# Low weight halves kept in DRAM, narrow products in a gated recurrence, and two deferred parts at another place

## The chip, the cores and the metric

The kernel runs on one core of one Trainium2 chip. The metric is the device time of one execution in microseconds (us). Engines are called PE (TensorE, matrix products), DVE (VectorE), ACT (ScalarE), POOL (GpSimd) and SP (SyncE, which only issues DMAs here).

## What is computed

Two sequences, a sample of 512 tokens and a prompt of 256, each of width 1024, go through the same two layers, all in float32:

```python
def trunk(x, ...):
    for l in range(DEPTH):                       # 2
        if l == 0: mix = ab_mixer(x, ...)        # HGRN heads beside dilated attention, output product
        else:      mix = conv_mixer(x, ...)      # gated product, 31-tap depthwise convolution
        x = layer_norm(ALPHA * x + mix, ...)
        x = layer_norm(ALPHA * x + sq_relu_mlp(x, mlp_w1[l], mlp_w2[l]), ...)

def sq_relu_mlp(x, w1, w2):
    return jnp.square(jax.nn.relu(x @ w1)) @ w2  # 1024 -> 4096 -> 1024

def conv_mixer(x, ...):
    a, gate = jnp.split(x @ w_in + b_in, 2, axis=-1)
    u = depthwise_conv(a * jax.nn.sigmoid(gate), dw_w, 31 taps) + dw_b
    return jax.nn.silu(layer_norm(u, n_g, n_b)) @ w_out + b_out
```

The HGRN mixer is a gated linear recurrence in both directions, over four heads of 128 channels: the state is decayed by a gate f and fed with k v at each token, and read with q.

## The kernel before

**Segments.** The sample is the long segment (`TS` = 512 columns, tiles 0 to 3, `segs` = `(0,)`), the prompt the short one (`TP` = 256, tiles 4 and 5, `segs` = `(1,)`). Most steps take one of them.

**Split products.** Weights and activations are split into a rounded high half (`wh`, `x0h`, `x1h`) and the low rest (`wl`, `x0l`, `x1l`), and a product is the sum of three: high by high, high by low, low by high. Weights come in units of 128 x 1024 (512 KB). `plan_units` lists them in the order of use. `advance` (lines 138 to 148) loads a unit into `raw` on SP's queue (line 143, three buffers), makes `wh` on ACT (line 135) and `wl` by a subtraction (line 136) on DVE, or on POOL for the units in `self.onpool`; these are all units from the convolution's first input product up to the second layer's MLP of both segments. `wh` and `wl` have five buffers each. `unit` hands one out and has the next three issued.

**HGRN.** For each head, `hgrn` builds the attention-like matrix `at` level by level for steps s of 1, 2, 4, ... 64 (`LEVELS`). At a level PE multiplies the keys by the queries (line 760 for s under 16, line 768 for s = 16, line 774 above), DVE copies the entries of that level from PSUM into `at` under a mask (line 778), and then `advance` of that function (lines 735 to 737) multiplies queries, keys and gate totals on, the forward direction on DVE and the backward one on POOL. For s under 16 a level is one product of 128 x 128 for each of six chunks, into a PSUM tile of its own, though the mask takes entries inside blocks of 2 s only. For s of 16 and more the products go to blocks inside one tile per segment (`ptop`). The input products of the next head run between the levels.

**First MLP layer.** `DEFER` is 8, so all eight chunks are first done for the long segment alone (from about 600 to 930 us), and then again for the short one, in twelve deferred parts: for each two chunks c and c+1 an `up c` (four units, products on line 168; ReLU and square on ACT, lines 940 to 942; the low half on DVE, line 943), an `up c+1`, and a `pair c` (eight units, products on line 980, sums on DVE, line 242). Each of the 64 units is so loaded and split twice.

**Where the parts stand.** `steps` writes the order: `MIX` says how many parts follow the first norm's middle and each two input products (`cin`) of the long segment's convolution, `NPOS` how many stand between the convolution's `center` and `norm` steps. What is left stands behind `norm`. The order before is: first norm with up 0; two `cin`, up 1, pair 0; two `cin`, up 2, up 3; two `cin`, pair 2; two `cin`, up 4, up 5, pair 4, up 6; `center`; up 7; `norm`; pair 6; then the short segment's norm and the output product `cout`. This order is a priority: a scheduler in the compiler builds each engine's queue by it and by when it reckons that the operands are there. `LOW` puts the convolution's taps 500 places back.

**Convolution.** 31 taps a channel tile on DVE (line 1021, the last on 1018), a running sum over tiles (line 1027). `do_center`: PE forms the mean (line 1037), DVE subtracts it (1041), ACT squares (1043), POOL and DVE add the squares (1048). `do_norm`: PE sums (1060), ACT takes the root (1064), DVE makes a diagonal (1067), PE spreads it (1070), and `channel_silu` (1079 to 1083, then the split into `x0h` and `x0l`) makes the operand of `cout` (line 182). The transposes of the norms are on line 232.

Of the kernel before, what the change touches and what calls it, by code (L numbers as in the profile page):

```python
# [20 lines left out]
P = 128  # L21
D = 1024
# [23 lines left out]
MIX = (1, 2, 2, 1, 4)  # L46
CMIX = (5,)
PT = "s"
NPOS = (0, 1)
# [51 lines left out]
class Kernel:  # L101
    def __init__(self, tc, ins, outs, ctx):
        self.tc, self.nc, self.i, self.o, self.ctx = tc, tc.nc, ins, outs, ctx
        self.n = 0
        self.post = False
        self.turn = 0
        self.mark = None
        self.flight = []
        self.x = [None, None]
        self.plan = []  # L110
        self.ready = {}
        self.issued = 0
        self.taken = 0
# [24 lines left out]
    def advance(self, upto):  # L138
        nc = self.nc
        while self.issued < min(upto, len(self.plan)):  # L140
            key, src = self.plan[self.issued]
            raw = self.sb(self.wp, [P, D], "raw", F32, RAW)
            nc.sync.dma_start(raw, src)
            hi = self.sb(self.wp, [P, D], "wh", F32R, WH)
            lo = self.sb(self.wp, [P, D], "wl", F32R, WL)
            self.split(raw, hi, lo, nc.gpsimd if self.issued in self.onpool else None)
            self.ready[self.issued] = (key, hi, lo)
            self.issued += 1
# [113 lines left out]
    def plan_units(self):  # L262
# [32 lines left out]
        self.onpool = set()  # L295
        win = False
        for step in self.steps():
            n0 = len(pl)
            if step[0] == "cin":
                win = True  # L300
            if step[2] == (0, 1):
                win = False
            {"up": up, "down": down, "pair": pair, "cin": conv_in, "cout": conv_out}.get(step[0], lambda *_: None)(*step[1])
            if win:
                self.onpool.update(n0 + q for q in range(len(pl) - n0))
# [402 lines left out]
    def hgrn(self, h, qs, ks, fs, gs, v):  # L708
# [31 lines left out]
        ptop = None  # L740
        for li, s in enumerate(LEVELS):
# [5 lines left out]
            for seg, (lo, hi) in enumerate(segs):  # L747
                if low or ptop is None or len(ptop) < 2:
                    pl = self.ps("s")
                    if not low:  # L750
                        ptop = (ptop or []) + [pl]
                else:
                    pl = ptop[seg]
                for c in range(lo, hi):
                    cc = slice(c * P, (c + 1) * P)
                    po = pl[:, (c - lo) * P : (c - lo + 1) * P]
                    if low:
                        rhs = bass.AP(tensor=qq.tensor, offset=qq.offset + c * P,
                                      ap=[qq.ap[0], [2 * s, P // (2 * s)], [T + s, 2], [1, s]])
                        nc.tensor.matmul(po, kc[:, cc], rhs, start=True, stop=True)  # L760
                        continue
# [438 lines left out]
```

## Time and profile before

| | us |
|---|---|
| median of 3 runs | 1906.98 (1906.2 to 1912.15) |
| profiled execution | 1907.15 |
| its span, first to last instruction | 1905.1 |
| granted clock of TensorE, mean | 0.987 |
| PE busy in the span | 1844.4 |
| DVE busy | 1146.5 |
| ACT busy | 738.2 |
| POOL busy | 603.3 |

Busy times of PE are modelled ends of pipelined products, so a busy PE can still be slow: the granted clock has to be read beside it. 1.00 is the level of 2.4 GHz, and a mean below 1.00 means that part of the stretch ran at 1.2 GHz.

### The profile page before, as it was taken

The page shows a single profiled execution, that of the slowest core. Times are in us where ns is not written, and L with a number is a line of the kernel's source. Part 1 is how long each engine was busy: PE and PEld are TensorE (multiplying, and loading weights), DVE is VectorE, ACT ScalarE, POOL GpSimd, SP SyncE. Part 2 cuts the span into 40 slices and gives each one's busy share as a digit, 9 for nine tenths or more (in the row PEclk, how much of TensorE's full clock was granted, in tenths as well). Part 3 has the DMA queues.
Part 4 walks back from the last instruction along what each step waited for, and adds up shares of the span by engine and source line. Part 5 has one row for each costly group of instructions (what it writes and reads, how often), then busy time and mean ns, then how long its engine had stood idle before and what let it go on. Part 6 is the DMA issues. An engine that isn't in the chain of part 4 may idle for free.

```text
span 1905.1 us, 26155 instructions
## 1 busy us (share of the span) xinstructions
PE 1844.4 (97%) x10516; PEld 1569.5 (82%) x10516; DVE 1146.5 (60%) x1813; ACT 738.2 (39%) x1200; POOL 603.3 (32%) x368
## 2 busy tenths in 40 slices
PE   8999999999999999999999999898999999999998
PEld 6798788887788888888789898688888789888886
DVE  4533527766766434334879999979993744333336
ACT  4423322334215333333444345544434545423322
POOL 4000105544310000000376668566445667000003
PEclk9999989999999999999999999899999999999999
DMA  7122221111213333333254444353332346321211
GB/s 234 34 72 74 65 89 45 34 45 35 100 48 122 107 93 92 108 100 95 72 157 149 148 145 155 122 155 107 94 99 89 129 159 194 116 67 59 64 44 66
DMA packets 56300, 189.57 MB, mean 100 GB/s; under 512 B 6979, under 2 KB 10099, under 8 KB 56180
## 3 DMA queue, kind: packets, MB, share of 16 engines
q1 hardware_dynamic: 52196, 177.23, 30.0%
q0 software_dynamic: 3120, 7.53, 1.4%
q10 hardware_dynamic: 864, 3.15, 0.5%
q8 instruction: 82, 1.34, 0.3%
q14 instruction: 38, 0.31, 0.1%
HBM read 182.49 MB, written 5.38 MB: 99 GB/s over the span
## 4 chain that ended last, share of the span: by engine, by line
PE 85%; DVE 11%; ACT 1%; issue 1%; POOL 1%; DMA 1%; SPq 0%; DVEq 0%; ACTq 0%; POOLq 0%
PE g L168 44%; PE s L182 25%; PE g L182 7%; PE s L980 3%; DVE qq L735 1%; DVE at L778 1%; DVE w L1082 1%; DVE x0l L136 1%; DVE g L736 1%; DVE r L242 1%; DVE x1l L136 1%; ACT wh L135 0%; DVE g L737 0%; DVE w L1083 0%; PE s L531 0%
## 5 line engine op out<-in xcount | busy, mean ns | idle before, releaser
L135 ACT ACTIVATE wh<-raw 128x1024 fp32r<-128x1024 f32 x320 | 339.2, 1061 | 731.8 <-PE g L168 304.8
L136 POOL TENSOR_TENSOR wl<-raw,wh 128x1024 fp32r<-128x1024 f32 x168 | 411.2, 2457 | 224.1 <-ACT wh L135 223.9
L182 PE MATMUL s<-wh,t 128*128 128x512 f32 x1280 | 398.1, 389 | 1.5 <-DVE r L242 1.5
L168 PE MATMUL g<-x0h,wh 128*128 128x512 f32 x864 | 339.6, 394 | 9.5 <-ACT wh L135 7.7
L168 PE MATMUL g<-x0l,wh 128*128 128x512 f32 x864 | 338.8, 392 | 0.2 <-DVE x0l L136 0.2
L168 PE MATMUL g<-x0h,wl 128*128 128x512 f32 x864 | 338.0, 391 | 0.0
L136 DVE TENSOR_TENSOR wl<-raw,wh 128x1024 fp32r<-128x1024 f32 x152 | 187.0, 1231 | 249.8 <-ACT wh L135 249.7
L182 PEld LDWEIGHTS s<-wh,t 128*128 128x128 f32 x1280 | 240.3, 188 | 52.1 <-DVE r L242 1.9
L1021 DVE SCALAR_TENSOR_TENSOR c<-t,vec,c 128x509 f32<-128x509 f32 (+26 forms) x464 | 250.2, 607 | 1.1
L182 PE MATMUL s<-wl,t 128*128 128x512 f32 x640 | 249.1, 389 | 0.0
L168 PE MATMUL g<-x1h,wl 128*128 128x256 f32 x864 | 246.9, 286 | 1.7 <-DVE wl L136 1.7
L168 PE MATMUL g<-x1l,wh 128*128 128x256 f32 x864 | 246.7, 286 | 0.3 <-DVE x1l L136 0.2
L168 PE MATMUL g<-x1h,wh 128*128 128x256 f32 x864 | 246.1, 286 | 0.1
L221 POOL TENSOR_TENSOR r<-r,lb 128x512 f32<-128x512 f32 x20 | 29.3, 1483 | 623.2 <-DVE r L220 623.2
L242 DVE TENSOR_TENSOR r<-r,s 128x512 f32<-128x512 f32 x164 | 112.3, 685 | 153.3 <-PE s L182 150.7
L168 PEld LDWEIGHTS g<-x0h,wh 128*128 128x128 f32 x864 | 162.5, 188 | 43.6 <-ACT wh L135 8.2
L168 PEld LDWEIGHTS g<-x0h,wl 128*128 128x128 f32 x864 | 162.5, 188 | 34.4 <-DVE wl L136 0.8
L168 PEld LDWEIGHTS g<-x0l,wh 128*128 128x128 f32 x864 | 162.7, 188 | 34.0 <-DVE x0l L136 1.4
L943 DVE TENSOR_TENSOR t<-t,t 128x512 fp32r<-128x512 f32 (+1 forms) x112 | 93.5, 835 | 138.4 <-ACT t L942 138.2
L168 PEld LDWEIGHTS g<-x1l,wh 128*128 128x128 f32 x864 | 167.4, 194 | 2.9 <-DVE x1l L136 0.7
L168 PEld LDWEIGHTS g<-x1h,wl 128*128 128x128 f32 x864 | 167.5, 194 | 2.2 <-DVE wl L136 2.0
L168 PEld LDWEIGHTS g<-x1h,wh 128*128 128x128 f32 x864 | 167.0, 194 | 2.8 <-ACT t L994 0.5
(335 smaller groups left out, 2522.4 us busy)
## 6 DMA issues: line engine op xcount, KB each, us to landing
raw<-w SPq DMA_DIRECT2D x224, 512.0 KB, 3.5
raw<-w_c SPq DMA_DIRECT2D x32, 512.0 KB, 3.7
raw<-w_a SPq DMA_DIRECT2D x16, 512.0 KB, 4.1
raw<-w_oc SPq DMA_DIRECT2D x16, 512.0 KB, 3.4
raw<-w_b SPq DMA_DIRECT2D x12, 512.0 KB, 9.9
raw<-w_oab SPq DMA_DIRECT2D x10, 512.0 KB, 3.5
raw<-w_vb SPq DMA_DIRECT2D x6, 512.0 KB, 3.4
r<-x ACTq DMA_DIRECT2D x6, 512.0 KB, 5.0
```

What stands on the lines that cost most here:

```text
L135: nc.scalar.activation(hi, src, AF.Copy)
L136: return (eng or nc.vector).tensor_tensor(lo, src, hi.bitcast(F32), ALU.subtract)
L168: mm = nc.tensor.matmul(p[:, 0:n], w, x[:, k, :], start=k == 0 and j == 0, stop=k == KD - 1 and j == 2)
L182: nc.tensor.matmul(out, a, w, start=k == 0 and j == 0, stop=k == n - 1 and j == 2)
L221: eng.tensor_tensor(half[q], half[q], b[q], ALU.add)
L242: self.nc.vector.tensor_tensor(dst, dst, p, ALU.add)
L735: eng.tensor_tensor(qv, qv, tv[:, :, kh : kh + 1].to_broadcast([P, n, s]), ALU.mult)
L736: eng.tensor_tensor(kv, kv, tv[:, :, qh : qh + 1].to_broadcast([P, n, s]), ALU.mult)
L778: nc.vector.copy_predicated(atv[:, lo:hi, :], m, pl[:, 0 : (hi - lo) * P].rearrange("p (c t) -> p c t", t=P))
L943: nc.vector.tensor_tensor(lo, rl, hi.bitcast(F32), ALU.subtract)
L980: self.nc.tensor.matmul(p, x, y, start=u == 0 and k == 0 and j == 0, stop=u == 3 and k == 1 and j == 2)
L1021: nc.vector.scalar_tensor_tensor(dst, src, tap, dst, ALU.mult, ALU.add)
```

## The change

The diff has three parts. In `advance`, a unit that is used again by the short segment's first MLP layer (`self.again`) has its `wl` stored in a DRAM tile by a DMA on POOL's queue when it is made; at its second use `wl` is loaded from there on SP's queue, right behind the `raw` load, and only `wh` is computed. In `hgrn`, levels 2, 4 and 8 multiply only the four diagonal blocks of 32 x 32 of each chunk, into the tile of level 1, which all levels of a segment now share. And `MIX` and `NPOS` move parts: behind the last two `cin` come up 4 and up 5 only; then `center`, pair 4, up 6, `norm`, up 7, pair 6.

```diff
-MIX = (1, 2, 2, 1, 4)
+MIX = (1, 2, 2, 1, 2)
-NPOS = (0, 1)
+NPOS = (0, 2)
...
             raw = self.sb(self.wp, [P, D], "raw", F32, RAW)
             nc.sync.dma_start(raw, src)
+            lo = self.sb(self.wp, [P, D], "wl", F32R, WL)
+            kept = self.kept.get(key)
+            if kept is not None:
+                nc.sync.dma_start(lo.bitcast(F32), kept)
             hi = self.sb(self.wp, [P, D], "wh", F32R, WH)
-            lo = self.sb(self.wp, [P, D], "wl", F32R, WL)
-            self.split(raw, hi, lo, nc.gpsimd if self.issued in self.onpool else None)
+            if kept is not None:
+                nc.scalar.activation(hi, raw, AF.Copy)
+            else:
+                self.split(raw, hi, lo, nc.gpsimd if self.issued in self.onpool else None)
+                if key in self.again:
+                    self.kept[key] = self.dram.tile([P, D], F32, tag="-".join(map(str, key)), name=self.name("kept"))
+                    nc.gpsimd.dma_start(self.kept[key], lo.bitcast(F32))
...
+            if step[0] in ("up", "down", "pair") and step[1][0] == 0 and step[2] == (1,):
+                self.again.update(key for key, _ in pl[n0:])
...
-                if low or ptop is None or len(ptop) < 2:
-                    pl = self.ps("s")
-                    if not low:
-                        ptop = (ptop or []) + [pl]
-                else:
-                    pl = ptop[seg]
+                if s == 1:
+                    ptop.append(self.ps("s"))
+                pl = ptop[seg]
...
-                    if low:
+                    if s == 1:
...
+                    if low:
+                        for b in range(P // 32):
+                            rr = slice(32 * b, 32 * b + 32)
+                            rhs = bass.AP(tensor=qq.tensor, offset=qq.offset + c * P + 32 * b,
+                                          ap=[qq.ap[0], [2 * s, 16 // s], [T + s, 2], [1, s]])
+                            nc.tensor.matmul(po[rr, rr], kc[:, cc][:, rr], rhs, start=True, stop=True)
                         continue
```

## Rows read from the trace of the kernel before

**Rows 1.** Table by stage: stretch, length, busy time (instructions), granted clock, DMA share, GB/s.
```profile
core 0: us, PE busy (x) PEld busy (x) DVE busy (x) ACT busy (x) POOL busy (x), PEclk, DMA share, GB/s
5.00:15.00 10.00, 7.22 (x20) 4.12 (x21) 7.28 (x14) 6.68 (x13) 2.25 (x4) 1.00 1.01 350
299.00:511.00 212.00, 197.64 (x1812) 170.69 (x1811) 157.01 (x243) 70.60 (x125) 103.25 (x101) 0.99 0.15 46
606.00:920.00 314.00, 313.97 (x1385) 259.54 (x1385) 131.33 (x157) 110.74 (x144) 2.87 (x2) 1.00 0.32 94
930.00:951.00 21.00, 16.76 (x114) 15.64 (x112) 19.04 (x28) 10.58 (x22) 8.06 (x4) 0.84 0.28 96
951.00:1160.00 209.00, 208.97 (x1148) 182.90 (x1149) 190.63 (x288) 93.72 (x133) 148.40 (x62) 1.00 0.49 151
1160.00:1264.00 104.00, 90.64 (x496) 76.07 (x494) 87.73 (x110) 57.84 (x85) 64.52 (x29) 0.92 0.41 128
```

**Rows 2.** Chain that ended last: start, length, engine, tile, line, products.
```profile
1072.50 21.76 PE s L980 x96
...
1568.55 11.51 PE g L168 x96
```

**Rows 3.** Page, costliest groups: the subtraction of a weight unit on either engine.
```profile
L136 POOL TENSOR_TENSOR wl<-raw,wh 128x1024 fp32r<-128x1024 f32 x168 | 411.2, 2457 | 224.1 <-ACT wh L135 223.9
...
L136 DVE TENSOR_TENSOR wl<-raw,wh 128x1024 fp32r<-128x1024 f32 x152 | 187.0, 1231 | 249.8 <-ACT wh L135 249.7
```

**Rows 4.** Timeline of PE, fourth head: start, length, work; levels 4, 8, 32.
```profile
479.24 1.05 PE L760 MATMUL s<-qq,mv 128*128 128x128 f32 x8
...
482.68 1.13 PE L760 MATMUL s<-qq,mv 128*128 128x128 f32 x8
...
484.01 0.47 PE L182 MATMUL g<-wh,x0l 128*128 128x512 f32 x1
...
490.73 0.46 PE L774 MATMUL s<-qq,g 128*32 128x32 f32 x32 [1.28 <-DVE g L736]
...
491.29 0.50 PE L182 MATMUL g<-wh,x0h 128*128 128x512 f32 x1
```

**Rows 5.** Timeline of POOL and DVE, first head, around level 4.
```profile
308.48 1.20 POOL L735 TENSOR_TENSOR qq<-qq,g 128x384 f32<-128x384 f32 x1
...
309.63 1.23 POOL L736 TENSOR_TENSOR g<-g,g 128x384 f32<-128x384 f32 x1
...
310.93 0.54 POOL L737 TENSOR_TENSOR g<-g 128x48 f32<-128x48 f32 x1
...
312.44 0.44 DVE L778 COPY_PREDICATED at<-mask,s 128x256 f32<-128x256 uint8 x1
...
312.78 0.54 DVE L735 TENSOR_TENSOR qq<-qq,g 128x384 f32<-128x384 f32 x1
```

**Rows 6.** Waits of PE, 925 to 951 us: us in total, times, longest.
```profile
PE s L232 <- DVE r L221: 2.1, 1, 2.1
PE g L168 <- DVE wl L136: 1.7, 1, 1.7
```

**Rows 7.** Waits of PE, 1160 to 1264 us.
```profile
PE s L182 <- ACT x0h L135: 4.1, 2, 3.6
PE c L1037 <- DVE y L1027: 3.7, 1, 3.7
```

**Rows 8.** Lines 1027 and 1082, 951 to 1235 us: min/median/max ns, first and last start.
```profile
L1027 DVE TENSOR_TENSOR y<-y,w x6: 686/1753/2828, 1062.4 to 1173.8; 128x512 f32<-128x512 f32 x6
...
L1082 DVE TENSOR_SCALAR w<-w,vec x8: 534/1508/2647, 1201.0 to 1228.1; 128x512 f32<-128x512 f32 x8
```

**Rows 9.** Timeline behind the centre, ACT, DVE and POOL.
```profile
1191.55 1.06 ACT L135 ACTIVATE wh<-raw 128x1024 fp32r<-128x1024 f32 x1 [2.74 <-DMA raw<-w]
...
1194.74 1.99 DVE L1067 TENSOR_TENSOR t<-ident,crs 128x512 f32<-128x512 f32 x1
...
1200.75 2.40 POOL L136 TENSOR_TENSOR wl<-raw,wh 128x1024 fp32r<-128x1024 f32 x1 [1.79 <-ACT wh L135]
...
1200.96 2.48 DVE L1082 TENSOR_SCALAR w<-w,vec 128x512 f32<-128x512 f32 x1
```

**Rows 10.** A DMA issue on POOL, and the page's loads of units (us to landing).
```profile
582.98 0.53 POOL L186 DMA_DIRECT2D lg<-ln  x1 [22.73 <-DVE r L212]
...
raw<-w SPq DMA_DIRECT2D x224, 512.0 KB, 3.5
```

More of the change, by code (lines that the diff above doesn't have):

```diff
@@ L112, in __init__ @@
         self.issued = 0
+        self.kept = {}
         self.taken = 0
@@ L295, in plan_units @@
         self.onpool = set()
+        self.again = set()
         win = False
@@ L738, in advance @@
             tot[d] = tv[:, :, 0]
-        ptop = None
+        ptop = []
         for li, s in enumerate(LEVELS):
@@ L760, in hgrn @@
                         nc.tensor.matmul(po, kc[:, cc], rhs, start=True, stop=True)
+                        continue
+                    if low:
[4 more added lines that the diff above has]
+                            nc.tensor.matmul(po[rr, rr], kc[:, cc][:, rr], rhs, start=True, stop=True)
                         continue
```

## The prediction, made before the changed kernel ran

> **What bounds the kernel now.** I read the table by stage first: PE is the bound nearly everywhere, and the reader should look for the stages in which its busy time falls short of the stretch or its granted clock falls short of 1.00 [rows 1]. In 606 to 920 us, the long segment's first MLP layer, PE is busy 313.97 of 314 us, and in 951 to 1160 us, the convolution's input products mixed with the short segment's parts, 208.97 of 209. Nothing that only relieves another engine can shorten these two. What is lost lies in three places. In 299 to 511 us, the four HGRN heads, 14.4 us of 212 are idle. In 930 to 951 us, the first norm, 4.2 us are idle at a clock of 0.84. In 1160 to 1264 us, centre, norm, SiLU and output product of the convolution, 13.4 us are idle, and at a clock of 0.92 another 8% of 104 us, 8.3, goes: 21.7 us together. The chain of waits then gives the pace of PE's work: a short up part of four weight units takes 11.51 us (2.88 a unit), a pair part of eight takes 21.76 (2.72 a unit) [rows 2].
>
> **HGRN levels.** Steps 2, 4 and 8 now issue 24 narrow products (128 rows, 32 columns) a head instead of 6 full ones: 12 levels in all, since there are four heads. A full level holds PE from 482.68 to 484.01, 1.33 us; the level of step 32 already has 24 products of just the new shape (48 records) and holds it from 490.73 to 491.29, 0.56 us [rows 4]. That is 0.77 us a level and 9.2 us over 12, if PE is what sets the level's length. It is not quite: between levels the other engines update their operands. Two levels begin 3.44 us apart (479.24 and 482.68) [rows 4]; without 0.77 this is 2.67, but POOL's three updates of one level run from 308.48 to 311.47, 2.99 us [rows 5]. With POOL as floor a level gives back only 0.45, 5.4 in all. The three levels now also write the PSUM tile that the level before left for the masked copy, so PE waits for that copy. DVE runs the copies before the update for which PE waits already (copy at 312.44, update at 312.78 [rows 5]), so I cost this at nothing; were the copy put behind the update, 0.44 us a level, 5.3 in all, would go and nothing would be left. I take 7 us, range 0 to 9.2.
>
> The Trainium skill, TensorE: Matmul & The Clock Gate, section on 56 against 53.3 ns, says that matmuls follow one another no closer than about 25 ns however narrow they are; by it 48 records need 1.2 us, a level gains 0.13 and the whole time would be near 1891. The trace disagrees: 32 records stand in 0.46 us, 14 ns each [rows 4].
>
> **Stores of the low halves.** In the long segment's pass each of the 64 units gets one more DMA, 512 KB from the `wl` tile to DRAM on POOL's queue. The issue holds POOL 0.53 us [rows 10], 34 us in a stretch of 314 in which POOL is busy 2.87 and DVE 131 [rows 1]. It waits for DVE's subtraction; queued behind it on POOL are only the first norm's additions. The tile is reused five units later and filled three units ahead of use; a unit lasts 5.4 us there (24 records at 21.76/96 [rows 2]), so a store has some 16 us, and no store is in the trace to show more than a load's 3.5 us [rows 10]. PE's full pace covers it: 0 us. If the cover were gone, it would show as gaps of PE in 606 to 920.
>
> **Loads in place of subtractions.** In the short segment's pass 64 subtractions vanish: 60 on POOL at 2.46 us and 4 on DVE at 1.23 [rows 3]; 64 loads on SP's queue take their place. PE never waits for POOL's, so their time itself is worth nothing. Two effects remain.
>
> First, the four on DVE lie in the first norm, where PE waits 1.7 us for one of them and 2.1 for the norm itself [rows 6]. The 1.7 goes at once; what is late next is the norm's own last addition on DVE. I take 2 us, range 0 to 3.8.
>
> Second, POOL's subtraction holds up DVE's operations on SBUF: the running sum takes 0.69 us alone and 2.83 at worst, the affine step of the SiLU 0.53 and 2.65 [rows 8]; the step at 1200.96 ends with POOL's subtraction that began at 1200.75 [rows 9]. Until 1160 PE hides this. After it, it is the path.
>
> **Centre, norm and SiLU.** The deferred parts total the same PE work, so PE's gain is what the 21.7 us of loss can give back. Before, the centre's product came after parts up 4, up 5, pair 4 and up 6; now pair 4 and up 6 are issued behind the centre, and up 7 and pair 6 behind the norm. The scheduler fills PE by readiness, so I expect the order on PE to change little, and the norm to come ahead of up 7 on ACT and DVE. Step by step: PE's wait of 3.7 us for the running sum [rows 7] goes, as its last two additions no longer meet a subtraction. ACT no longer stands 2.74 us on a raw half whose buffer POOL freed late [rows 9]; the root follows right behind it, and about 2.2 of this is on the path. The diagonal, 1.99 us under a subtraction [rows 9], falls towards 0.7: 1.3. Two SiLU steps under the short parts' last subtractions lose some 1.9 each: 3.8. One more for up 7's operations behind the norm. Sum 12 us. The output product's own four subtractions stay on POOL and go on holding up DVE, so the wait of 4.1 us for the first `x0h` [rows 7] stays in part: this is what is late next. Range 3.7 (the first wait alone) to 21.7 (the whole loss).
>
> **Can the loads keep up?** A kept unit moves 1.049 MB, so PE asks for 385 GB/s in a pair part and 364 in an up part. The queues moved 151 GB/s at a share of 0.49, 308 at full share, and 350 at a share of 1.01 in 5 to 15 us [rows 1]. At 308 a unit takes 3.40 us. Behind the last input product 32 units follow in 89.6 us of PE work (4 x 11.51 + 2 x 21.76); the loads need 108.8, 19.2 more. Five buffers give a lead of four units, 11.2 us, so 8 us are left, and they fall due in the stretch in which some 10 us of loss remain anyway. The shorter bursts (12, 8 and 8 units) fit in the lead. The other lead that goes: SP issues a `wl` load only when its buffer is free, and the next raw half stands behind it. I cost both at 0, range 0 to 8.
>
> **Sum.** The profiled execution took 1907.15 us (span 1905.1, 2 us around it), the median of the runs is 1906.98: the same within 0.2. 1907.15 - 7 - 2 - 12 = 1886. The ends: 1907.15 - 3.7 = 1903.5, or 1911 with the 8 us of loads in full; 1907.15 - 34.7 = 1872.5. Faster and slower are counted from 0.3%, 5.7 us, about what a measurement can tell.
>
> **The rivals.** *Only the plain waits go.* POOL keeps the levels long (5), the first norm gives 1, and the centre gives its 3.7: 1897. For it: the output product's subtractions still meet the SiLU. Against it: ACT's stand on the raw half is plain in the trace. *All goes well*: near 1873. *Narrow products don't run side by side*: a level then gains nothing, 1907 - 2 - 12 = 1893; the 14 ns between records speak against it, and the page named above is its only support. *Given back later:* up 7 and pair 6 end later, the short segment's norm waits for their sums behind the SiLU on DVE, and the stage returns its 12 while the levels give 4: 1903, no change that can be told. For it: DVE is busy 87.7 of 104 us there [rows 1]. *Slower, the loads starve PE:* at 250 GB/s a unit takes 4.19 us; the burst of 32 comes 44.5 us behind PE, less the lead of 11.2 and 10 us of loss that remain anyway 24, the burst of 12 adds 6: 30 us, 1916. It eats the whole gain from about 262 GB/s down. For it: a share of 0.49 leaves room for twice the present 151 GB/s, the short parts ask for 2.4 times, and the loads of one unit stand in line on one queue. Against it: 350 over ten microseconds. *That nothing is kept* I exclude: both passes use the same keys.
>
> **How the numbers follow.** Forecast 1886 (its own range 1878 to 1895) 0.46; plain waits 1897, 0.20; all well 1873, 0.08; narrow products 1893, 0.03; given back 1903, 0.11; starved 1916, 0.12. Faster by over 0.3%: 0.46 + 0.20 + 0.08 + 0.03 = 0.77; within 0.11; slower 0.12. The range 1872 to 1908 leaves out the starved case, the upper part of the one before and a little below: under 0.2.
>
> **What would show it.** Levels of steps 2 to 8 hold PE some 0.6 us, and 299 to 511 shrinks by 7. The `wl` loads of the short pass land without a wait of PE for them; DMA's share in 951 to 1160 nears 1. The running sum's last addition is near 0.7 us, PE's wait at the centre is gone, ACT takes no 2.7 us before the root, and PE in 1160 to 1264 loses 10 us instead of 21.7. It is wrong if PE waits for `wl` or `wh` in the short parts, if 951 to 1160 grows, or if the levels stay 3 us or more apart.

## The result and the profile after

The changed kernel takes 1891.02 us (median of 4 runs, 1890.05 to 1893.42) against 1907.74 (4 runs, 1906.2 to 1912.15) for the kernel before beside it: a ratio of 0.9911, 95% interval 0.9891 to 0.993, so 13 to 21 us less. The forecast was 1886, with 1872 to 1908 as its range. The profiled execution is the one of 1891.02 us, its span 1889.2.

The table by stage of the changed kernel comes first, in the columns of [rows 1]: the HGRN heads, the long segment's first MLP layer, the first norm, the convolution's input products with the short parts, and the stretch from the running sum's end to the output product's.

```profile
core 0: us, PE busy (x) PEld busy (x) DVE busy (x) ACT busy (x) POOL busy (x), PEclk, DMA share, GB/s
299.00:504.00 205.00, 186.75 (x2230) 159.03 (x2230) 152.06 (x238) 67.76 (x122) 104.35 (x99) 0.99 0.15 47
599.00:913.00 314.00, 313.97 (x1385) 259.67 (x1384) 132.02 (x158) 112.42 (x148) 32.67 (x58) 1.00 0.61 197
913.00:944.70 31.70, 24.12 (x164) 21.91 (x164) 29.65 (x40) 19.46 (x32) 16.28 (x8) 0.92 0.59 199
944.70:1155.00 210.30, 210.30 (x1151) 183.84 (x1150) 183.75 (x288) 90.26 (x128) 28.78 (x12) 1.00 0.73 256
1155.00:1248.00 93.00, 87.31 (x496) 74.97 (x494) 69.07 (x110) 58.40 (x87) 32.21 (x16) 0.96 0.65 221
```

The MLP layer is as full as before although POOL now issues the stores. The input products lose nothing. (Line numbers are each kernel's own: lines 168, 182, 760, 980, 1027 and 1082 of before are 178, 192, 770, 997, 1044 and 1099 here, and the narrow products are on 777.) The last stretch idles 5.7 us and runs at a mean clock of 0.96, another 3.7: 9.4 us, where 21.7 went before. The first norm got worse: 7.6 us idle of 31.7, where 4.2 were idle before [rows 1].

What the page says of the weight units, subtractions first, then DMAs with the median us to landing:

```profile
L137 POOL TENSOR_TENSOR wl<-raw,wh 128x1024 fp32r<-128x1024 f32 x108 | 264.6, 2464 | 291.7 <-ACT wh L136 191.9
...
L137 DVE TENSOR_TENSOR wl<-raw,wh 128x1024 fp32r<-128x1024 f32 x148 | 182.1, 1231 | 244.4 <-ACT wh L136 241.5
...
kept<-wl POOLq DMA_DIRECT2D x64, 512.0 KB, 5.5
wl<-kept SPq DMA_DIRECT2D x64, 512.0 KB, 4.7
```

POOL has 60 subtractions fewer than in [rows 3], DVE 4 fewer; 64 stores and 64 loads stand in their place.

To set kernels beside one another I cut each profile at the same products of PE: the first product of the first head's recurrence, the first of the MLP, the last of the MLP's long segment, the first input product of the convolution, the centre's, the last of pair 6, and the first product behind the output product. Lengths in us; the HGRN column goes on from the four heads to the MLP, and the last column is the sum from the first input product on, taken from unrounded marks. Left out are the MLP's long segment, 350.2 or 350.3 in every kernel, and all behind the output product (650.4 before, 650.6 after).

| kernel | ahead of the heads | HGRN | first norm | inputs to centre | centre to pair 6 | output product | convolution |
|---|---|---|---|---|---|---|---|
| before | 299.7 | 278.1 | 22.5 | 226.6 | 42.5 | 35.3 | 304.6 |
| after | 297.2 | 273.5 | 23.8 | 223.5 | 44.6 | 25.9 | 294.2 |
| hgrn_only | 297.3 | 274.3 | 22.5 | 226.6 | 43.3 | 37.5 | 307.6 |
| kept_only | 303.9 | 278.0 | 23.9 | 224.6 | 35.9 | 32.8 | 293.5 |
| place_only | 298.3 | 278.4 | 22.5 | 226.6 | 58.5 | 25.5 | 310.8 |
| kept_place | 297.8 | 277.8 | 23.8 | 224.8 | 43.1 | 25.8 | 293.8 |
| pool_busy | 297.8 | 274.5 | 25.5 | 224.6 | 52.9 | 28.6 | 306.4 |
| pool_long | 298.8 | 273.1 | 26.0 | 228.2 | 56.5 | 27.1 | 312.0 |
| up0_split | 298.7 | 274.1 | 22.5 | 222.8 | 41.6 | 25.8 | 290.5 |
| more_kept | 303.7 | 273.3 | 21.8 | 223.2 | 41.6 | 27.3 | 292.3 |
| lo_poolq | 298.6 | 274.5 | 22.9 | 223.4 | 42.2 | 25.6 | 291.4 |
| no_copies | 296.6 | 282.4 | 23.8 | 224.0 | 41.7 | 26.0 | 291.9 |
| tot_dve | 296.4 | 276.1 | 21.6 | 222.8 | 41.6 | 26.0 | 290.6 |
| twice | 300.5 | 272.9 | 17.7 | 241.5 | 77.3 | 27.3 | 346.4 |

Two things are to be seen. The first column is code that no kernel changes, and it varies from 296.4 to 303.9: a total taken from one profile is good to some 4 us only. Stages of equal code spread less: the HGRN column is 277.8 to 278.4 with the full products and 272.9 to 274.5 with the narrow ones (no_copies and tot_dve, which change the levels further, left aside), and the convolution is 304.6 and 307.6 in before and hgrn_only, 294.2 and 291.9 in after and no_copies. So a difference of one pair tells something from about 2 us up in HGRN and from about 3 us up in the convolution. And of the 15.9 us between the spans of before and after, HGRN gave 4.6 and the convolution 10.4; the first norm took back 1.3, and 2.5 lay in that first column.

### The profile page after: what moved, and what is told of

It is laid out like the page before. It is cut to its first block, busy times and chain, and to the rows that moved or that the text cites. A ratio compares the mean times of both kernels' runs of the same rounds, so it can differ in the third digit from the quotient of the medians.

```text
span 1889.2 us, 27170 instructions
## 1 busy us (share of the span) xinstructions
PE 1828.8 (97%) x10948; PEld 1556.0 (82%) x10948; DVE 1121.0 (59%) x1809; ACT 737.2 (39%) x1200; POOL 492.9 (26%) x372
## 4 chain that ended last, share of the span: by engine, by line
PE 86%; DVE 9%; ACT 2%; issue 1%; POOL 1%; DMA 1%; DVEq 0%; SPq 0%; ACTq 0%; POOLq 0%
PE g L178 45%; PE s L192 25%; PE g L192 7%; PE s L997 3%; DVE qq L748 1%; DVE at L795 1%; DVE g L749 1%; ACT wh L136 1%; DVE r L230 1%; DVE r L252 1%; DVE x1l L137 0%; PE s L544 0%; PE c L544 0%; PE s L597 0%; DVE r L946 0%
## 5 line engine op out<-in xcount | busy, mean ns | idle before, releaser
L136 ACT ACTIVATE wh<-raw 128x1024 fp32r<-128x1024 f32 x256 | 271.4, 1060 | 614.4 <-PE s L192 285.8
L137 POOL TENSOR_TENSOR wl<-raw,wh 128x1024 fp32r<-128x1024 f32 x108 | 264.6, 2464 | 291.7 <-ACT wh L136 191.9
L137 DVE TENSOR_TENSOR wl<-raw,wh 128x1024 fp32r<-128x1024 f32 x148 | 182.1, 1231 | 244.4 <-ACT wh L136 241.5
L960 DVE TENSOR_TENSOR t<-t,t 128x512 fp32r<-128x512 f32 (+1 forms) x112 | 85.7, 765 | 142.9 <-ACT t L959 142.7
L192 PEld LDWEIGHTS s<-wl,t 128*128 128x128 f32 x640 | 120.2, 188 | 24.6
```

Source lines behind the costliest of these rows:

```text
L136: nc.scalar.activation(hi, src, AF.Copy)
L137: return (eng or nc.vector).tensor_tensor(lo, src, hi.bitcast(F32), ALU.subtract)
L192: nc.tensor.matmul(out, a, w, start=k == 0 and j == 0, stop=k == n - 1 and j == 2)
L960: nc.vector.tensor_tensor(lo, rl, hi.bitcast(F32), ALU.subtract)
```

## The experiments

### The parts of the change one by one

**hgrn_only**: the kernel before with the narrow products and the shared PSUM tile of the diff's second half, nothing else.

> The narrow products of levels 2, 4 and 8 alone, in the kernel before. Theory (PE's shorter levels are worth what the stage showed): the stretch from the first head to the first MLP layer is 7 us shorter, all behind it only shifted: 1900 to 1901 us. Rival (the 7 us came from a changed order around the heads, not from the products): under 3 us, 1904 or more. The levels of steps 2 to 8 should hold PE about 0.6 us in either case.

1903.13 us, ratio 0.9978 (0.9964 to 0.9992). The stage gains 3.8 us (278.1 to 274.3), not 7. All kernels with full products set against all with narrow ones, the gain is 3.3 to 5.5. The later convolution came out 3.0 us longer in this profile, with no edit there.

**kept_only**: the kernel before with the stores and loads of the low halves alone.

> The stored low halves alone, with the parts and the HGRN levels as before. Theory (POOL's subtractions held up DVE and freed raw halves late): the convolution's tail gains most of its 11 us, 8 to 10, and the first norm loses 1 to 2: about 1899. Rival (the place of the parts brought it): the tail gains 3.7 us at most, 1903 to 1906. The first norm's loss of 1.7 us must be here, if it comes from the loads.

1895.17, ratio 0.9941 (0.9924 to 0.9959). The convolution gains 11.1 us, the first norm loses 1.4.

**place_only**: the kernel before with

```diff
-MIX = (1, 2, 2, 1, 4)
+MIX = (1, 2, 2, 1, 2)
-NPOS = (0, 1)
+NPOS = (0, 2)
```

> The two parts moved alone, all weights split as before. Theory (lock and raw halves are the cause): under 3 us gained, 1904 to 1907, the last running sum still near 2.8 us. Rival (the norm ahead of up 7 on ACT and DVE is the cause): 6 us or more, 1901 or less.

1911.69, ratio 1.0031 (1.0018 to 1.0045): slower, which neither theory had. PE's waits of this kernel in 1150 to 1262 us (us in total, times, longest) say where:

```profile
PE s L980 <- POOL wl L136: 4.1, 3, 2.1
PE s L980 <- DVE t L943: 4.0, 2, 2.8
...
```

The pair products (L980) now wait 4.0 us for the low half of an up part's output (L943), which stands behind norm and SiLU on DVE, and 4.1 for subtractions. The stretch from centre to pair 6 grows by 16 us; the output product, whose weights are then ready, gives 9.8 of them back.

**kept_place**: both of these, without the narrow products.

> Stored low halves and moved parts without the narrow products. If the parts add up, this is the changed kernel's 1891.0 and 7 us: 1898. If the moved parts only pay once POOL is free, it is faster than the sum of the two alone by some us: kept_only and place_only would then add to less than 9 us.

1893.68, ratio 0.9939 (0.9918 to 0.9959), beside 0.9941 for the kept halves alone. The placement is worth nothing that can be measured on top of them: pair 6 ends 7.2 us later (43.1 against 35.9), and the output product is 7.0 shorter. The parts nearly add: 0.9978 times 0.9939 is 0.9917, measured 0.9911.

### What the subtractions cost

**pool_busy**: the changed kernel, with work on POOL for each kept unit of the convolution's stage that no product waits for; POOL is held for some 2.6 us a unit, in four pieces.

```diff
             if kept is not None:
                 nc.scalar.activation(hi, raw, AF.Copy)
+                if self.issued in self.onpool:
+                    idle = self.sb(self.ap, [P, 256], "idle", bufs=1)
+                    for q in range(4):
+                        hq = hi[:, 256 * q : 256 * q + 256].bitcast(F32)
+                        nc.gpsimd.tensor_tensor(idle, hq, hq, ALU.subtract)
```

> The changed kernel, but at each kept unit that POOL split before, POOL subtracts the high half from itself in four operations of 256 columns, into a tile that nobody reads; raw halves stay free of it. Theory (POOL holds up DVE's operations on SBUF): DVE's additions of the running sum, the affine steps and line 960 are stretched again, the convolution's tail loses 5 to 10 us, 1896 to 1901. Rival (what counted were raw halves freed earlier and the shorter chain load, split, use): under 2 us lost, 1893 or less, though DVE's operations look longer.

1906.45, ratio 1.0002 (0.9988 to 1.0015): the gain is gone, so it came from POOL's free time and not from the weights' being ready sooner (PE's wait for high halves is 2.4 us here as in the changed kernel). But the running sum, which I had taken for the mechanism, is stretched little (below: minimum, median and maximum in ns, 944 to 1235 us):

```profile
L1049 DVE TENSOR_TENSOR y<-y,w x6: 685/852/1100, 1061.4 to 1171.2; 128x512 f32<-128x512 f32 x6
```

What grew are waits for POOL's own queue, here PE's in 1150 to 1262 us:

```profile
PE c L1082 <- POOL t L1070: 4.1, 1, 4.1
...
PE s L197 <- POOL wl L137: 2.2, 3, 1.0
PE s L1002 <- DVE t L965: 2.2, 2, 1.8
```

L1070 is POOL's part in adding the squares. In this order of steps POOL's additions stand among the idle pieces; without these, PE waits 0.8 us there, and 0.2 instead of 2.2 for the output product's subtractions. These waits for POOL's own results grew by 5.3 us, those for DVE (L965 and the running sum) by 2.7. The stretch is not quite gone: DVE is busy 254.7 us in the convolution here, 247.5 in the changed kernel. Whether a full stretch costs more is what the next run asks.

**pool_long**: the same occupation in one piece, written over the raw half, which nothing reads any more.

```diff
                 nc.scalar.activation(hi, raw, AF.Copy)
+                if self.issued in self.onpool:
+                    nc.gpsimd.tensor_tensor(raw, raw, hi.bitcast(F32), ALU.subtract)
```

> The changed kernel with one idle subtraction of 128 x 1024 on POOL for each kept unit that POOL would have split, written over the raw half, which nothing reads any more: POOL is as occupied as in the run with four idle operations of 256 columns, but in one piece of some 2.45 us, as before the change. No product waits for it. Theory A (DVE's operations on SBUF stand still while POOL's run, so the length of POOL's piece is what matters): the running sum and the SiLU's affine step are stretched to 2 us and more again, and the stage from the first input product to the output product's end takes 306 us or more, the time is 1906 to 1912. Theory B (POOL's own queue is what matters: its squares and additions stand behind the idle work): the stage takes the same 306 us as with the short pieces, and the waits that grow are those for POOL's squares. Theory C (neither: what counted in the other run was the high half held until POOL was done, or the quadrupled number of operations): the stage is near 294 to 298 and the time 1891 to 1897.

1910.8, ratio 1.0022 (1.0012 to 1.0031). The running sum is stretched as in [rows 8]:

```profile
L1046 DVE TENSOR_TENSOR y<-y,w x6: 684/1456/2781, 1061.7 to 1175.2; 128x512 f32<-128x512 f32 x6
```

and PE's waits in 1150 to 1262 us are

```profile
PE s L999 <- DVE t L962: 7.6, 1, 7.6
PE c L1079 <- POOL t L1067: 4.7, 1, 4.7
PE c L1056 <- DVE y L1046: 2.8, 1, 2.8
```

DVE is busy 269.6 us in the convolution, which takes 312.0 us, 5.6 more than with the short pieces. The waits that grew are for DVE: 2.8 instead of 0.5 for the running sum, and 7.6 instead of 2.2 for an up part's low half. The chain of waits shows what stands ahead of that low half, affine steps (L1101) and products of the SiLU (L1102), two of which take 0.99 and 1.28 us where POOL is idle:

```profile
1207.53 3.02 DVE w L1101 x2
1210.55 5.53 DVE w L1102 x2
```

Against after's 294.2, POOL's occupation in short pieces costs 12.2 us, and their joining into long ones 5.6 more. Not all of the 12.2 is waiting: PE's idle time in the convolution grows by 7.9 us, and its busy time, at a lower mean clock (0.97 instead of 0.98), by 4.4. By the waits, 5.3 against 2.7 us, the larger cause in the short pieces is POOL's own queue; that long ones also cost by stretching DVE is what the chain above shows. One qualification: the long piece also holds the raw half until POOL is done, as a subtraction does, which the short ones do not. ACT waits 9.5 us for raw halves of kept units here, 6.7 with the short pieces and 4.4 in the changed kernel; no run separates what this adds to the 5.6. Place_only, which has the real subtractions in the same order of steps, takes 310.8.

The Trainium skill, SBUF — State Buffer, section on who interferes with whom, calls the pair of SBUF ports that DVE and POOL share an exclusive lock, held for a whole instruction by whichever came first. The runs agree: one and the same sum takes 0.68 us alone, at most 1.10 beside pieces of 0.61 us, and up to 2.78 beside pieces of 2.41 (medians of the pieces).

### The first norm

**up0_split**: the changed kernel, with the low halves of up 0 computed a second time instead of loaded.

```diff
-            if step[0] in ("up", "down", "pair") and step[1][0] == 0 and step[2] == (1,):
+            if step[0] in ("up", "down", "pair") and step[1][:2] != (0, 0) and step[1][0] == 0 and step[2] == (1,) or step[0] == "pair" and step[1] == (0, 0):
```

> The changed kernel with the four units of part up 0 split on DVE twice, as before, not kept. Theory (in the first norm the loads let PE use up 0 too early and bring POOL's subtractions for the first input products, 10.99 us in a row, onto the norm's scaling on DVE): the stretch from the last MLP product to the first input product goes back from 23.9 to 22.5 us, the whole to 1889 to 1890. Rival (the loads of that stretch are late by themselves, or it is chance): 23.9 stays.

1886.4 (1886.03 to 1897.08), ratio 0.991 (0.9883 to 0.9937). The norm is back at 22.5 us, as before the change, and the convolution is 3.7 shorter. Of the latter, 3.0 lie between centre and pair 6, and there it is PE's clock: from 1170 to 1190 us PE is busy 19.22 us in both kernels, at 0.83 in the changed one and at 1.00 here, behind 15 us in which both had it busy throughout. The runs don't show why it fell in the one and not in the other. The times cannot tell this kernel from the changed one, 0.9911: the stages of one profile gain some 5 us, the two medians differ by 4.6, and the intervals cover one another.

What went wrong in the changed kernel is seen in PE's waits of 905 to 946 us, and in DVE and POOL at that time (timeline: start, length, engine, line):

```profile
PE s L242 <- DVE x0l L137: 4.0, 1, 4.0
PE s L242 <- DVE r L231: 3.0, 1, 3.0
```

```profile
930.40 5.71 DVE L230 TENSOR_TENSOR r<-r,lg 128x512 f32<-128x512 f32 x2
936.03 3.43 DVE L231 TENSOR_TENSOR r<-r,lb 128x512 f32<-128x512 f32 x2
```

```profile
927.46 10.86 POOL L137 TENSOR_TENSOR wl<-raw,wh 128x1024 fp32r<-128x1024 f32 x4 [2.91 <-ACT wh L136]
```

With no subtraction between them, up 0's units pass more quickly, and the first input products' units follow sooner. Their four subtractions on POOL now fall on the norm's scaling on DVE: two scalings take 5.71 us and two shifts 3.43. In up0_split, where POOL has only two subtractions by then and is done at 933.8, it is

```profile
934.87 1.28 DVE L230 TENSOR_TENSOR r<-r,lg 128x512 f32<-128x512 f32 x2
```

and as much for the two shifts. And up 0, which would have been PE's work in that pause, is already done.

### The levels of HGRN

In [rows 4] and here, PE's timeline shows when a level begins. This is the first head of the changed kernel, steps 2, 4 and 8 (L777) and 16 (L785):

```profile
303.64 0.46 PE L777 MATMUL c<-qq,e 128*32 128x32 f32 x31
...
304.19 0.50 PE L178 MATMUL g<-x0l,wh 128*128 128x512 f32 x1
...
307.68 0.43 PE L777 MATMUL c<-qq,mv 128*32 128x32 f32 x29 [1.16 <-DVE qq L748]
...
310.92 0.43 PE L777 MATMUL c<-qq,mv 128*32 128x32 f32 x29 [0.88 <-DVE qq L748]
...
313.69 0.50 PE L785 MATMUL c<-qq,g 128*32 128x16 f32 x37
```

A level holds PE for 0.55 us (303.64 to 304.19), as forecast. Yet step 4 begins 4.04 us after step 2 and step 8 3.24 after step 4, to the hundredth what it was before. Step 16 comes 2.77 after step 8 instead of 3.20, and is itself 1.67 longer (4.43 instead of 2.76). From step 1's first product to step 64's it is 22.08 us in the changed kernel, and was 21.55: as a whole the levels did not shorten. The gain lies behind them, as the next two tables show: before, from step 1 to step 64, and from there to the next head; then the same two stretches after.

```profile
300.95:322.50 21.55, 18.80 (x247) 15.89 (x246) 19.48 (x29) 5.10 (x10) 14.66 (x16) 1.00 0.10 26
322.50:356.66 34.16, 33.64 (x234) 29.68 (x234) 19.87 (x30) 13.34 (x22) 12.13 (x11) 1.00 0.16 47
```

```profile
298.41:320.49 22.08, 18.25 (x364) 14.75 (x364) 20.58 (x31) 4.99 (x10) 15.64 (x16) 1.00 0.16 50
320.49:352.60 32.11, 31.40 (x224) 28.15 (x225) 18.44 (x28) 13.11 (x22) 12.17 (x11) 1.00 0.11 34
```

In the first stretch PE ran 53 of the next head's input products before and runs 62 now; in the second 139, and now 130. Three levels freed 2.3 us of PE, and nine products of some 0.23 us, 2.1 us, moved up into that. Over both stretches PE's busy time falls by 2.8 us (52.44 to 49.65) and its idle time rises by 1.3 (3.27 to 4.54): 1.5 us are left. The heads gain 1.5, 1.3, 1.2 and, the last, behind which no head's products are left to pull up, 0.5. PE's waits in the levels name the updates (L748 to L750) and never a masked copy: the tile that the levels now share cost nothing, as forecast.

Who does pace the levels? Two runs.

**no_copies**: the changed kernel without the masked copies of steps 2, 4 and 8.

```diff
-                if low or s == 64:
+                if s == 1 or s == 64:
```

> The changed kernel without the masked copies of HGRN levels 2, 4 and 8 (six copies a head, 3.5 us of DVE; the entries of these levels are left out of the result). Theory A (DVE ends the wait: copies, then the update, and PE waits for the copies through the shared tile): a level shortens by most of its 1.18 us of copies, 8 to 14 us over 12 levels, 1877 to 1883. Theory B (POOL's three updates are the floor, as the prediction took it): under 3 us, 1888 or more.

1900.1, ratio 0.9974 (0.996 to 0.9988): slower than the changed kernel by 9 us, with less to do. Three things happened. With DVE freed of its copies, the first four levels of the first head last 5.22, 3.84, 3.07 and 2.38 us instead of the changed kernel's 5.23, 4.04, 3.24 and 2.77, and from step 1 to step 64 it is 20.8 instead of 22.1. PE's waits there change for the larger part from DVE to POOL (299 to 504 us; before this edit, 8.8 us of those on L777 were DVE's):

```profile
PE c L777 <- POOL qq L748: 6.3, 4, 2.1
PE s L777 <- DVE qq L748: 4.0, 2, 2.1
PE s L777 <- POOL qq L748: 3.3, 2, 2.1
```

So POOL's updates are hardly shorter than what DVE had. The other two things cost more: the scheduler built another order, and PE's clock fell. The first lines are the table of no_copies, the second of the changed kernel, over the same steps:

```profile
302.00:307.00 5.00, 2.90 (x61) 1.83 (x63) 4.83 (x5) 1.46 (x3) 4.76 (x6) 0.99 0.22 85
307.00:314.00 7.00, 6.38 (x199) 4.65 (x200) 5.13 (x8) 0.52 (x1) 4.11 (x4) 0.52 0.01 2
```

```profile
302.00:307.00 5.00, 4.49 (x65) 3.14 (x63) 4.86 (x7) 1.48 (x3) 4.76 (x5) 1.00 0.28 98
307.00:314.00 7.00, 5.44 (x160) 4.88 (x162) 6.53 (x13) 1.57 (x3) 4.06 (x5) 1.00 0.01 2
```

In no_copies the order that the scheduler built leaves PE idle for 2.1 of the 5 us, and in the next 7 the granted clock is 0.52, that is 1.2 GHz nearly throughout; in the changed kernel, PE is busy 4.49 of these 5 and stays at 2.4. In its order only 41 input products of the next head stand between the levels, instead of 62, and at the lower level one came 0.43 us behind the other instead of 0.23. The rest had to be made up behind the levels, where 28.7 us now pass from line 829's first product to the next head instead of 24.7. Over the HGRN stage PE's busy time grows by 6.3 us (253.8 to 260.1, at a mean clock of 0.96 instead of 0.99) and its idle time by 2.5. What the order and what the clock is worth by itself, no run separates.

**tot_dve**: up0_split with the backward direction's gate totals of the first four steps on DVE instead of POOL.

```diff
+            eng = nc.vector if s < 16 else eng
             eng.tensor_tensor(tv[:, :, 0], tv[:, :, 0], tv[:, :, 1], ALU.mult)
```

> The kernel with up 0's low halves computed, and the backward direction's gate totals of steps 1, 2, 4 and 8 multiplied on DVE instead of POOL: POOL loses 16 operations of 0.53 to 0.85 us, and its three updates of a level become two of 2.4 us together, while DVE gets 16 more of 0.2 to 0.8 us. Theory A (POOL's own three updates are the floor of a level): two levels of a head begin 2.6 to 2.8 us apart instead of 3.2, the HGRN stage falls from 274.1 to 266 to 270 us, and the time is 1879 to 1883. Theory B (DVE is as near to the floor, since its operations stretch under POOL's, or the exchange of the totals between the two engines costs a wait a level): levels stay 3.1 to 3.3 apart or more, the stage is 273 to 278 us, the time 1885 to 1890.

1891.72 (1886.55 to 1892.52), ratio 0.9918 (0.9904 to 0.9931). The stage takes 276.1 us, 2.0 more than in up0_split: theory B. The levels of the first head begin 5.83, 4.41, 2.67 and 2.99 us apart, where it was 5.23, 4.08, 3.22 and 2.76: three longer, one shorter. From step 1 to step 64 it is 22.03 us, and was 22.10. The first three heads take as long as in up0_split or up to 0.4 us less; the longer time lies in the last head and behind it. POOL's queue alone is not the floor: work taken from it and given to DVE leaves the sum where it was. In the changed kernel's first head DVE is busy 20.6 of these 22.1 us and POOL 15.6 (above), so DVE is at least as near to the floor.

### The loads

**twice**: the changed kernel, with each kept half loaded two times into the same tile.

```diff
                 nc.sync.dma_start(lo.bitcast(F32), kept)
+                nc.sync.dma_start(lo.bitcast(F32), kept)
```

> The changed kernel with each kept low half loaded twice into the same tile, so that a kept unit moves 1.573 MB instead of 1.049. Theory A (the DMA queues' rate of some 350 GB/s, the most that any row has shown, is a ceiling, and the changed kernel lies below it with its 256 GB/s in the convolution's input stage): that stage now asks for some 27 MB more in 210 us, about 385 GB/s, so it grows by 20 us or more, PE waits for low or high halves in the short parts, and the time is 1911 to 1931. Theory B (one queue's loads of several units run beside one another and the ceiling is far above 350): no wait of PE for a weight, the stage stays within 3 us of 223.5, and the time is 1889 to 1895. Under A the rival of loads that starve PE was a matter of half as many bytes again; under B it was never near.

1939.18, ratio 1.017 (1.0154 to 1.0187). The first line is this kernel's table, behind it PE's waits in 944 to 1260 us:

```profile
1208.00:1238.00 30.00, 22.97 (x136) 21.04 (x135) 13.48 (x26) 19.53 (x36) 0.00 (x0) 0.89 0.95 358
```

```profile
PE s L998 <- DMA wl<-kept: 14.5, 10, 2.9
...
```

Theory A, and more than it had: the queues are full, PE waits for low halves, and the convolution takes 52 us more (46 together with the first norm, which is shorter here). But 358 GB/s is not yet the ceiling: from 1155 to 1185 us this kernel moves 376 at a share of 1.00. Nor did the changed kernel lie far below it. It moves 256 GB/s on the mean of its input products, and around their end this:

```profile
1141.50:1171.50 30.00, 30.00 (x191) 27.07 (x191) 27.02 (x46) 14.92 (x23) 0.00 (x0) 1.00 0.99 375
```

For 30 us its queues are full too, and PE is busy all the same. A kept unit's 1.049 MB take 2.80 us at this rate, just the pace of PE's short parts (2.72 to 2.88 us a unit). The rival of loads that starve PE was real, and it was missed by next to nothing in these 30 us; with half as many bytes again it came. The Trainium skill, Perfetto Trace Analysis, section Engine Utilization, gives 358 GB/s as a core's share of the memory's peak; its Roofline note there lets a lone core go beyond, to some 435. The traces agree with the note: 375 over 30 us here, and 413 over 20 us in pool_long (585 to 605, stores beside loads); none shows 435 for so long.

**lo_poolq**: the changed kernel with these loads on POOL's queue.

```diff
-                nc.sync.dma_start(lo.bitcast(F32), kept)
+                nc.gpsimd.dma_start(lo.bitcast(F32), kept)
```

> The changed kernel with the kept low halves loaded on POOL's queue, so that raw halves on SP's queue no longer stand behind a load that waits for a free buffer. Theory (the line on SP's queue is what is late now: PE waits 2.4 us for high halves in pair 6, and the output product's raw halves come at 1198 to 1210): the tail from centre to the short segment's input products loses 2 to 5 us, 1886 to 1889. Rival: POOL now stands at a free buffer itself, its squares and subtractions come late, or its descriptors meet DVE: no gain, 1891 to 1895.

1893.69, ratio 0.9938 (0.9923 to 0.9953). The convolution is 2.8 us shorter and the norm 0.9, but the rest behind the convolution, with no edit in it, came out longer in that profile (654.3 us, not 650.6), and the run shows no gain. It tells that PE's wait for high halves in pair 6, below, does come from SP's queue: these 2.4 us are gone here. But PE now waits 1.9 us there for an up part's low half on DVE, and its idle time from centre to pair 6 is 3.5 us where it was 3.7: what is late next takes the place of what went. That stretch is 2.4 us shorter by PE's clock (0.96 instead of 0.92), and the output product is as long as in the changed kernel (25.6 and 25.9).

**more_kept**: up0_split, and the short segment's input and output products take their low halves from DRAM too.

```diff
+            if step[0] in ("cin", "cout") and step[2] == (1,):
+                self.again.update(key for key, _ in pl[n0:])
```

> A version for speed: up 0's low halves are computed, as in the run that did this alone, and the short segment takes the low halves of the convolution's input and output products from DRAM too, where the long segment's pass stored them. Theory A (a subtraction on POOL costs time wherever DVE or POOL's own additions are on the path): the short segment's convolution has no subtraction left on POOL and gains some us behind its input products: 1880 to 1884. Theory B (PE hides them there, and the loads of 1.049 MB a unit come back to back without other work between): no gain over 1886.4, or a loss of some us where PE waits for a raw half behind the loads, 1886 to 1892.

1888.82 (1887.8 to 1890.0), ratio 0.991 (0.9893 to 0.9926): the same as the changed kernel and as up0_split. The input products' stretch moves 298 GB/s here at a share of 0.84, and up to the centre POOL is busy 41.8 us, in 28 instructions, where up0_split has 33.8 in 14: the added stores. No version beats the changed kernel by what the runs can tell.

## Why the prediction held, and which of its steps did not

The time lies in the range, but that range, 1872 to 1908, also held four of the rivals (1897, 1873, 1893 and 1903), and the one of 1893 (narrow products one behind the other) came nearer to 1891 than the forecast of 1886 did. So the terms have to be looked at one by one.

**HGRN, forecast 7, measured 4.6 and 3.8.** The term was mis-sized: the prediction's own value with POOL as floor, 5.4, was nearer, and the mechanism was another. The step that failed is "0.77 us a level, if PE is what sets the level's length", together with POOL as the floor. PE's hold of a level is 0.55 us as forecast, but most levels stay 3 us or more apart, which the prediction had named as a sign of its failure. The saving is paid out elsewhere, as products of the next head pulled up, and only as far as there are any. Who paces the levels is shown only as far as this: neither the copies taken from DVE nor the totals taken from POOL shorten them by more than 1.3 us of 22. Narrow products do run side by side, against the rival of 1893: 48 records lie in 0.55 us, 11 ns each, where a quarter of a full level's hold (1.33 us for 12 records) would be 28.

**First norm, forecast -2, measured +1.3.** Wrong in sign. The step "the 1.7 goes at once; what is late next is the norm's own last addition" saw PE's wait and not what it kept apart. Loading up 0's halves let the next units through earlier, onto the norm.

**Stores at 0** held: 56 issues of 0.53 us in the stretch, and PE 313.97 of 314. They land in 5.5 us (median, 10.5 at most), more than the 3.5 I had a row for, and within the 16 that a tile stays.

**Loads at 0** held: from 944.7 to 1155 us PE has no wait. The step "308 at full share" had the rate too low: at a share of 0.99 the loads moved 375 GB/s, which is what the parts behind the last input product ask for (364 and 385), so the shortfall of 19.2 us that the prediction set against buffers and loss did not arise. The rival needed 262 GB/s or less. The share nears 1 only there, as the input products lie between the parts before; its mean up to 1155 is 0.73. (In the rival's sum, 44.5 less 11.2 and 10 is 23, not 24; nothing hangs on it.)

**Convolution, forecast 12, measured 10.4.** The loss behind the running sum fell from 21.7 to 9.4 us, where 10 had been forecast to be left; with the spread of kernels that share the convolution's code the gain is 10.4 to 15.7, so the size is not contradicted. The signs came as named: running sum and affine step are no longer stretched (944 to 1235 us): eight affine steps take 0.54 us each, and of the sums the profile says

```profile
L1044 DVE TENSOR_TENSOR y<-y,w x6: 677/680/693, 1057.3 to 1167.0; 128x512 f32<-128x512 f32 x6
```

The diagonal takes 0.69, and PE's waits of 1155 to 1250 us are these:

```profile
PE s L997 <- ACT wh L151: 2.4, 3, 1.5
PE s L242 <- DVE x1l L137: 1.7, 1, 1.7
PE c L1077 <- POOL t L1065: 0.8, 1, 0.8
...
```

What is left out are two of 0.5 us or less. The 3.7 for the running sum and the 4.1 for `x0h` of [rows 7] are gone. Two steps of the term's working did not hold. First, 8.8 of the 12 us (3.7, 1.3 and 3.8) were DVE's stretching, and POOL's own queue was put at nothing ("PE never waits for POOL's"). In pool_busy the gain is gone with about a third of the stretch (DVE's 7.2 us in the convolution beside 22.1 in pool_long), and of the waits that came back 5.3 us are for POOL's results and 2.7 for DVE's; so 12 came out near for partly the wrong reason. Second, "the output product's four subtractions go on holding up DVE": they come later, behind the SiLU, and what is late there is their raw halves, though PE loses only 0.2 us in the output product by it. SP's queue and then the chain of waits show it (start, length, what):

```profile
1189.02 3.04 SPq L148 DMA_DIRECT2D wl<-kept  x2
1194.65 2.10 SPq L144 DMA_DIRECT2D raw<-w  x2
...
1197.90 6.87 SPq L144 DMA_DIRECT2D raw<-w_oc  x3
```

```profile
1203.37 1.05 ACT wh L151
...
1204.44 3.10 DMA raw<-w_oc
1207.54 2.41 POOL wl L137
```

A `wl` load waits on SP for a free buffer, and every raw half stands behind it: the "other lead that goes", which the prediction had named and costed at 0. PE's wait of 2.4 us for `wh` (L997, pair 6), which lo_poolq does not have, comes from it; lo_poolq gained nothing by its going, so 0 stands. From 1160 to 1240 us SP waited 25.5 us for PE to free such a buffer. It waited longer for raw buffers, 32.0 us on POOL's subtractions and 10.8 on ACT, as in the chain above; before, 65.7 on POOL.

**The placement**, credited with part of the 12 (norm ahead of up 7), is worth nothing on top of the kept halves and costs 5.9 us without them (by the ratio; 3.4 to 8.6). The step "the norm comes ahead of up 7 on ACT and DVE" was right as an order, but what it displaces, up 7's low half, is what pair 6 waits for.

**The sum.** 7 + 2 + 12 = 21 was forecast; 4.6 - 1.3 + 10.4 = 13.7 is what the stages show. The runs' 16.7 is more than these explain. In these two profiles all three terms gave less than forecast. That the total came no further off is in part chance: 2.5 us of the profile's 15.9 lie ahead of the heads, in code that no edit touches. Whether the change itself sets that start lower stays open: other kernels with the same code have it anywhere in 7.5 us.

## What to carry to other kernels

When work is taken from an engine that seldom holds anyone up directly, ask two things of it: whose operations stand behind it in its own queue, and whose it stretches; an idle dummy of the same size, in one piece and in several, helps to tell the two apart. Shortening the products of a dependent chain gains only as much other work as there is to pull into the freed gaps. And a wait that goes lets the next stage's units start earlier: look at what they then fall on.

## What the hardware showed that was not expected

Taking work away made a kernel slower: in no_copies, 5 us in which PE was busy 2.90 were followed by 7 at 0.52 of the full clock, in the first head, and its HGRN stage took 8.9 us more than the changed kernel's, in part by the clock and in part by another order of products. The clock also fell, to 0.83 for 20 us, in one of two kernels whose PE was equally busy before and in these 20 us (the changed kernel and up0_split), which made some 3 us of difference between them.

Loads of whole units held 375 GB/s at a share of 0.99 over 30 us without one wait of PE; with half as many bytes again the convolution lost 52 us. A full queue cost nothing as long as it kept PE's pace, and there was no room above it: 376 at 1.00 is the most that the doubled loads reached over 30 us.
